# A two-branch attention block on one core: the instruction order planned with another model of the shared port, and another last norm

## The chip, the cores and the metric

The program runs on one core of a Trainium2 chip, alone. The metric is the device time of one execution in microseconds. The kernel before was timed three times: 430.37, 432.68 and 432.4 us, median 432.4 us. The engines are TensorE (PE, with its weight loads PEld), VectorE (DVE), ScalarE (ACT), GpSimd (POOL) and SyncE (SP, which only issues DMAs).

## What is computed

One residual layer on 512 tokens of width 1024, in float32, cut to what matters here:

```python
h = rmsnorm(x, norm_g)
q_lat, c_kv, k_rope, z_a, q_b, k_b, v_b, z_b, q_idx, k_idx, w_idx, gate_a, gate_b = split(h @ w_in)
# branch A: 8 heads, low-rank latents, dense chunk-causal softmax
q = rmsnorm(q_lat, g_q_lat) @ w_uq;  kv = rmsnorm(c_kv, g_kv_lat) @ w_ukv
y_a = mla_attention(q, kv, rope(k_rope)) * silu(z_a)
# branch B: an indexer scores the keys, each query keeps its best 128, 8 heads with a bias by distance
score = sum_h relu(q_idx[h] @ k_idx.T / sqrt(32)) * w_idx[h] / sqrt(8)
y_b = dsa_attention(q_b, k_b, v_b, top_k(score, 128), rel_bias) * silu(z_b)
merged = sigmoid(gate_a) * (y_a @ w_o_a) + sigmoid(gate_b) * (y_b @ w_o_b)
out = rmsnorm(x + merged @ w_out, final_g)
```

## The kernel before

Every float32 operand of a large product is split into a rounded high part and the rest, and a product is three matmuls (high by high, high by low, low by high; `mm3`). The split is two instructions: ACT rounds (a CAST, written `act`), and DVE or GpSimd subtracts (`lo_part`, a TENSOR_TENSOR). Work is tiled in 128 rows by up to 512 columns; `s0` to `s72` are SBUF slots of 128x512 that all stages share, `raw` four larger buffers for weights that arrive, `ps` the eight PSUM banks. In the names of the trace and of the order, what stands behind an underscore (`s_w`, `s_latraw`) is what the slot holds.

The stages in time: the input, its latents (`latent`: the q latent 384 wide and the kv latent 256 wide, scaled per token and turned by TensorE transposes) and the indexer's q and k; then gates and projections of the normed input, which serve as filling work, beside branch A's heads, the scores of the indexer (`scores`, L841 in the trace) and the choice of the best keys (`topk`, MAX8 and MATCH_REPLACE on DVE); then branch B's heads; then the products with `w_o` and, by a seven-product scheme, with `w_out`; then the last norm (`finish`, `square`, `scale_out`), token tile by token tile, tile 1 last.

Nothing of the order is left to a scheduler at run time. The program is written as some sixty generators, each yielding steps, and a planner (`Flow`) runs them against a model of the chip: a step has a list of engines that could do it with a duration each, the model knows when an engine, a buffer and the shared port are free (`start`, `run`), and the step with the smallest key is emitted next. So the order on each engine is a result of the model's numbers. Each engine then executes its own list strictly in order and waits on semaphores; a wrong guess of the model becomes a wait that holds everything behind it on that engine.

Three parts of the model bear on the change. DVE steps with `pair` (two SBUF inputs, or a fast scaling) and POOL's computing steps share one port: `port` is the time at which the last of them ends, and another may start only then. A choice between engines is biased by `PEARLY`, `pbias` and, after the last top-k, by `LATE`. A thread has a priority, weighted by `BIAS` and for POOL by `YIELD`.

GpSimd also issues some DMAs itself (`pool_dma`, L466: tables, and with `QPOOL = 1` the first of three copies that build each of the indexer's eight q tiles `s_qs`; the other two go through SP, L462). `small_pow` (L402, L410) makes 1/sqrt of a mean for four token tiles: on GpSimd one multiply-add and one power.

In the last norm each half row (tile `t`, half 0 or 1) is read out of PSUM by DVE into `s_xr` (L371), squared and summed by ACT (for the last piece by DVE, L1807), and multiplied by `final_g` (`s_fg`). For half 1, and for tile 1, DVE first makes `s_rg` = row by gain by sqrt(1024), and the scale by 1/norm follows; for half 0 of tiles 0, 2 and 3 DVE does both at once, after the norm is known, and stores `s_xr`.

Of the kernel before, what the change touches and what calls it, by code (L numbers as in the profile page):

```python
# [150 lines left out]
class Flow:  # L151
# [126 lines left out]
def tile_block(ctx: ExitStack, tc: tile.TileContext, a: dict, out: bass.AP, bias_dram: bass.AP):  # L278
# [121 lines left out]
    def small_pow(dst, src, mul):  # L400

        yield Step([("POOL", 0.17, lambda: nc.gpsimd.tensor_scalar(dst.ap, src.ap, mul, EPS, ALU.mult, ALU.add))],  # L402
# [83 lines left out]
    def pool_dma_out(dst, src):  # L486
        step = Step([("POOL", 1.03, lambda: nc.gpsimd.dma_start(dst, src.ap))], [], bufs(src))
# [385 lines left out]
    def bias_table():  # L873
        yield is_done("loads")
# [922 lines left out]
    def finish(t, half, c0, c1, ps, nth, last, keep=False):  # L1797

        r = xr[t, half].all.f[:, c0:c1]
# [4 lines left out]
        if last:  # L1804
# [7 lines left out]
            done.add(("sum", t))
        else:
            spawn(square(t, r, nth), 0)
# [298 lines left out]
```

## Time and profile before

| | |
|---|---|
| runs | 430.37, 432.68, 432.4 us; median 432.4 us |
| the profiled execution | 432.45 us, of which the span of the profile is 430.7 us |
| granted TensorE clock, mean | 0.995 |
| PE busy | 418.3 us, 97% of the span |
| DVE, ACT, POOL busy | 380.3, 258.9, 96.0 us |
| HBM read, written | 50.49 MB, 4.21 MB |

The profile is one execution. Times in its rows are microseconds from the span's start. A timeline row gives the start, the time from the first start to the last end of equal neighbours, the engine and line, the operation, what is written and read, the shape and the count; in brackets the idle time before and what ended it. SPq, POOLq and ACTq are the issuing sequencers; DMA_DIRECT2D is the issue of a DMA. Matmuls are pipelined and their ends are modelled, so that idle time of PE in the rows is less than what a wait costs; the distance from start to start is the better measure.

### The profile page before, as it was taken

The page shows a single profiled execution, that of the slowest core. Times are in us where ns is not written, and L with a number is a line of the kernel's source. Part 1 is how long each engine was busy: PE and PEld are TensorE (multiplying, and loading weights), DVE is VectorE, ACT ScalarE, POOL GpSimd, SP SyncE. Part 2 cuts the span into 40 slices and gives each one's busy share as a digit, 9 for nine tenths or more (in the row PEclk, how much of TensorE's full clock was granted, in tenths as well). Part 3 has the DMA queues.
Part 4 walks back from the last instruction along what each step waited for, and adds up shares of the span by engine and source line. Part 5 has one row for each costly group of instructions (what it writes and reads, how often), then busy time and mean ns, then how long its engine had stood idle before and what let it go on. Part 6 is the DMA issues. An engine that isn't in the chain of part 4 may idle for free.

```text
span 430.7 us, 7067 instructions
## 1 busy us (share of the span) xinstructions
PE 418.3 (97%) x2305; PEld 363.5 (84%) x2305; DVE 380.3 (88%) x818; ACT 258.9 (60%) x585; POOL 96.0 (22%) x118
## 2 busy tenths in 40 slices
PE   9999989999999999999999999999999999999993
PEld 6999768789887888888899987998988888888883
DVE  5778699999999999899677899998899858999996
ACT  5786766658492857658363665674489524346623
POOL 2043746434444444300003001000020000000312
PEclk9999999999999999999999999999999999999997
DMA  8973334634425563372443435255333786548305
GB/s 266 395 262 107 101 102 130 176 118 116 149 67 144 160 154 98 85 217 73 129 135 118 148 119 132 75 153 145 87 98 123 263 325 223 187 158 278 107 2 195
DMA packets 30277, 65.89 MB, mean 153 GB/s; under 512 B 4648, under 2 KB 5688, under 8 KB 30240
## 3 DMA queue, kind: packets, MB, share of 16 engines
q1 hardware_dynamic: 29120, 63.82, 47.7%
q0 software_dynamic: 832, 1.22, 1.1%
q8 instruction: 18, 0.29, 0.3%
q10 hardware_dynamic: 288, 0.39, 0.2%
q14 instruction: 19, 0.16, 0.1%
HBM read 50.49 MB, written 4.21 MB: 127 GB/s over the span
## 4 chain that ended last, share of the span: by engine, by line
PE 51%; DVE 25%; ACT 7%; issue 7%; DMA 5%; POOL 2%; SPq 1%; POOLq 0%; DVEq 0%; ACTq 0%
PE ps L435 45%; PE ps L452 3%; ACT s_p L338 2%; DVE sm L863 2%; DVE mask L864 2%; DMA s_op<-s_op 2%; DVE mask L371 2%; DMA s_raw<-onehot 1%; DVE s_wo L360 1%; DVE s_mg L360 1%; DVE s_pair L360 1%; DVE sm L1513 1%; DVE s_w L360 1%; SPq L462 1%; DVE s_ph L360 1%
## 5 line engine op out<-in xcount | busy, mean ns | idle before, releaser
L435 PE MATMUL ps<-s_h,s_w 128*128 128x512 f32 (+1 forms) x732 | 171.5, 379 | 0.0
L435 PEld LDWEIGHTS ps<-s_h,s_w 128*128 128x128 f32 x732 | 127.8, 189 | 21.6 <-issue 0.2
L329 ACT CAST s_w<-raw 128x512 fp32r<-128x512 f32 (+3 forms) x124 | 71.7, 593 | 28.0 <-DVE raw L360 14.0
L362 POOL TENSOR_TENSOR s_w<-raw,s_w 128x512 fp32r<-128x512 f32 (+2 forms) x34 | 41.5, 1227 | 154.9 <-ACT s_w L329 100.8
L360 DVE TENSOR_TENSOR s_w<-raw,s_w 128x512 fp32r<-128x512 f32 (+2 forms) x90 | 58.1, 661 | 7.7 <-ACT s_w L329 7.4
L435 PE MATMUL ps<-s_ys,s_w 128*128 128x512 f32 x192 | 43.7, 389 | 0.0
L435 PEld LDWEIGHTS ps<-s_ys,s_w 128*128 128x128 f32 x192 | 36.0, 188 | 7.5
L435 PE MATMUL ps<-s_w,s_xg 128*128 128x328 f32 (+1 forms) x192 | 32.9, 324 | 0.2 <-ACT s_rbc L329 0.2
L435 PE MATMUL ps<-s_wo,s_mg 128*128 128x512 f32 (+1 forms) x156 | 33.0, 373 | 0.0
L435 PEld LDWEIGHTS ps<-s_wo,s_mg 128*128 128x128 f32 x156 | 27.6, 188 | 5.2
L435 PEld LDWEIGHTS ps<-s_w,s_xg 128*128 128x128 f32 x192 | 31.4, 188 | 0.6 <-ACT s_rbc L329 0.5
L338 ACT ACTIVATE s_p<-s_p,sm 128x256 f32<-128x256 f32 (+3 forms) x50 | 27.2, 560 | 7.8 <-DVE sm L1610 7.8
L338 ACT ACTIVATE s_p<-ps,sm 128x128 f32<-128x128 f32 (+3 forms) x32 | 16.7, 525 | 15.7 <-DVE sm L1513 15.5
L864 DVE MATCH_REPLACE8 mask<-sm,mask 128x256 f32<-128x256 f32 (+2 forms) x48 | 25.8, 540 | 0.0
L863 DVE MAX8 sm<-mask 128x8 f32<-128x256 f32 (+2 forms) x48 | 25.1, 547 | 0.1
L452 PE MATMUL ps<-ident,s_p 128*128 128x128 f32 x160 | 22.8, 273 | 0.0
L329 ACT COPY s_tmp<-ps 64x512 f32<-64x512 f32 (+1 forms) x18 | 10.1, 562 | 18.9 <-PE ps L435 18.8
L435 PE MATMUL ps<-s_lat,s_w 128*128 128x512 f32 x78 | 21.0, 397 | 0.0
L452 PEld LDWEIGHTS ps<-ident,s_p 128*128 128x128 f32 x160 | 18.6, 140 | 2.5
L435 PE MATMUL ps<-s_hs,s_w 128*128 128x256 f32 x144 | 20.0, 285 | 0.0
L360 DVE TENSOR_TENSOR s_ph<-ps,s_ph 128x512 fp32r<-128x512 f32 (+1 forms) x32 | 18.5, 611 | 0.6 <-ACT s_ph L329 0.6
L435 PEld LDWEIGHTS ps<-s_hs,s_w 128*128 128x128 f32 x144 | 18.4, 191 | 0.2
(198 smaller groups left out, 759.1 us busy)
## 6 DMA issues: line engine op xcount, KB each, us to landing
raw<-w_out SPq DMA_DIRECT2D x18, 512.0 KB, 4.2
s_op<-s_op SPq DMA_DIRECT2D x36, 128.0 KB, 2.4
raw<-w_ga SPq DMA_DIRECT2D x8, 512.0 KB, 4.6
raw<-w_gb SPq DMA_DIRECT2D x8, 512.0 KB, 3.8
raw<-w_o SPq DMA_DIRECT2D x16, 256.0 KB, 5.4
s_x<-xT SPq DMA_DIRECT2D x8, 256.0 KB, 4.9
s_xn<-x SPq DMA_DIRECT2D x8, 256.0 KB, 5.6
bias_scratch<-s_sig SPq DMA_DIRECT2D x8, 256.0 KB, 3.7
```

Of the source, the lines that this page charges most:

```text
L329: nc.scalar.copy(dst.ap, src.ap)
L338: nc.scalar.activation(dst.ap, src.ap, func, **kw)
L360: opts.append(("DVE", 0.07 + 0.00104 * x.n, lambda: nc.vector.tensor_tensor(dst.ap, x.ap, y.ap, op=op)))
L362: opts.append(("POOL", 0.15 + 0.0021 * x.n, lambda: nc.gpsimd.tensor_tensor(dst.ap, x.ap, y.ap, op=op)))
L371: lambda: nc.vector.scalar_tensor_tensor(dst.ap, x.ap, sc(s), y.ap, op0=op0, op1=op1))],
L435: nc.tensor.matmul(ps.ap, l.ap, r.ap, start=start and i == 0, stop=stop and i == len(pairs) - 1, skip_group_check=more)
L452: nc.tensor.transpose(d.ap, s.ap, ident.tile)
L462: return Step([("SP", n / 360000.0, lambda: nc.sync.dma_start(d, s))], bufs(dst), bufs(src))
L863: yield Step([("DVE", t, lambda: nc.vector.max(m8.tile, work.tile))], [m8], [work])
L864: yield Step([("DVE", t + 0.068, lambda: nc.vector.match_replace(work.tile, m8.tile, work.tile, MARK))], [work], [m8])
L1513: yield Step([("DVE", 0.07 + 0.00104 * n, lambda: nc.vector.tensor_reduce(mx.tile[:, 1:2], ps.tile[:, :n], op=ALU.max, axis=AX.X, negate=T ...
```

## The change

Five things change. The first is the model of the port: a step that would take the port from the other engine while it is still held, or is free for less than 0.01, is marked down by `SWITCH`, so that the holder's next step goes first; `BIAS` is halved.

```diff
-        self.port = 0.0
+        self.port, self.holder = 0.0, None
...
+                        change = SWITCH * (self.shares(t.req, eng) and eng != self.holder and s < self.port + 0.01)
+                        key = (max(s, self.due) + change + BIAS * t.prio + t.off + YIELD * self.shares(t.req, eng) * (eng == "POOL"), t.prio)
...
-                    self.port = end
+                    self.port, self.holder = end, eng
...
-BIAS = 0.004
+BIAS = 0.002
...
+SWITCH = 0.1
```

The second is GpSimd's DMAs: an issue costs the model 0.53 in place of 1.03, and a load from DRAM lands 2.5 later; no copy of the q tiles goes through GpSimd (`QPOOL = 0`), and the bias table begins when the rope keys are done (`BIAS_AT`) in place of when the loads are issued. Other numbers of the planner change with them.

```diff
-        step = Step([("POOL", 1.03, lambda: nc.gpsimd.dma_start(dst.ap, s))], bufs(dst), bufs(src))
+        step = Step([("POOL", 0.53, lambda: nc.gpsimd.dma_start(dst.ap, s))], bufs(dst), bufs(src))
+        step.late = 0.0 if isinstance(src, View) else 2.5
...
-        yield is_done("loads")
+        yield is_done("loads", BIAS_AT)
...
-QPOOL = 1
+QPOOL = 0
...
-PTOPK = 18.0
+PTOPK = 12.0
...
-LATE = 1.5
-PSUMS = 4.0
+LATE = 0.75
+PSUMS = 10.0
...
+BIAS_AT = 'kpe'
```

The third is the norm: the multiply-add of `small_pow` may be done by ACT or DVE, no longer by GpSimd.

```diff
-        yield Step([("POOL", 0.17, lambda: nc.gpsimd.tensor_scalar(dst.ap, src.ap, mul, EPS, ALU.mult, ALU.add))],
+        yield Step([("ACT", 0.1, lambda: nc.scalar.activation(dst.ap, src.ap, AF.Copy, scale=mul, bias=EPS)),
+                    ("DVE", 0.1, lambda: nc.vector.tensor_scalar(dst.ap, src.ap, mul, EPS, ALU.mult, ALU.add))],
                    bufs(dst), bufs(src))
         yield power(dst)
```

Both the second and the third show in GpSimd's list. Here is what stands there before, from the norm of the kv latents (`sm_78`) to that of the q latents (`sm_80`) and the first subtractions of weights:

```order
L402 TENSOR_SCALAR sm_78<-sm_77 128x4
L410 TENSOR_TENSOR sm_78<-sm_78,neghalf 128x4
L466 DMA s_qs_700<-s_th_510 32x384
L393 TENSOR_SCALAR s_latraw_519<-s_latraw_519,sm_78 128x256
L393 TENSOR_SCALAR s_latraw_530<-s_latraw_530,sm_78 128x256
L402 TENSOR_SCALAR sm_80<-sm_79 128x4
L410 TENSOR_TENSOR sm_80<-sm_80,neghalf 128x4
L362 TENSOR_TENSOR s_th_751<-s_tmp_748,s_th_750 128x384
L466 DMA s_qs_774<-s_th_750 32x384
L362 TENSOR_TENSOR s_w_757<-raw_67,s_w_756 128x384
L362 TENSOR_TENSOR s_w_799<-raw_67,s_w_798 128x384
```

And the same place after (lines have moved by two or three: 413 is the power, 469 the DMA, 395 the scaling, 364 the subtraction):

```order
L413 TENSOR_TENSOR sm_78<-sm_78,neghalf 128x4
L469 DMA s_raw_497<-chunk 4x512
L469 DMA qhi_72<-s_oh_498 4x512
L469 DMA qhi_73<-s_oh_498 4x512
L469 DMA qhi_74<-s_oh_498 4x512
L469 DMA qhi_75<-s_oh_498 4x512
L413 TENSOR_TENSOR sm_80<-sm_80,neghalf 128x4
L395 TENSOR_SCALAR s_latraw_716<-s_latraw_716,sm_80 128x384
L395 TENSOR_SCALAR s_latraw_734<-s_latraw_734,sm_80 128x384
L395 TENSOR_SCALAR s_latraw_751<-s_latraw_751,sm_80 128x384
L364 TENSOR_TENSOR s_w_769<-raw_67,s_w_768 128x384
L364 TENSOR_TENSOR s_w_803<-raw_67,s_w_802 128x384
```

The two multiply-adds and the copies to `s_qs` have left GpSimd; three of the four scalings of the q latents came to it (before, DVE did three and ACT one), ahead of the subtractions of weights; the kv latents are scaled by ACT.

SP's list has the eight copies more. Where branch B's first head is made ready (`s_op` are its operands, built of copies of the rope keys `kpeh`, `kpel` and of rotated values), it reads before:

```order
L462 DMA s_op_1640<-s_op_1623 64x512
L462 DMA raw_66<-w_kb 128x1024
L462 DMA s_op_1642<-s_op_1625 64x512
L462 DMA s_op_1572<-s_qpe_994 32x512
L462 DMA qhi_73<-s_qpe_993 32x512
L462 DMA s_op_1604<-s_qpe_994 32x512
L462 DMA s_op_1623<-kpeh 36x512
L462 DMA s_op_1625<-kpel 32x512
```

And after:

```order
L465 DMA s_op_1625<-s_op_1571 64x512
L465 DMA s_op_1532<-kpeh 36x512
L465 DMA bias_scratch<-s_sig_1675 128x512
L465 DMA s_op_1571<-kpel 32x512
L465 DMA s_op_1596<-kpeh 36x512
L465 DMA s_op_1625<-kpel 32x512
L465 DMA raw_66<-w_kb 128x1024
```

The load of `w_kb`, which stood among the copies, stands behind them; the store of a bias tile, `s_sig`, stands among them.

TensorE's list is rearranged between the latents and the end of branch A. One place, the scores of the indexer late in it, among the matmuls of a projection (`s_h`), before:

```order
L841 MATMUL ps_96<-s_qs_715,s_qs_880 128x384
L841 MATMUL ps_95<-s_qs_715,s_qs_774 128x512
L435 MATMUL ps_94<-s_h_543,s_w_950 128x512
L435 MATMUL ps_94<-s_h_544,s_w_950 128x512
L435 MATMUL ps_94<-s_h_543,s_w_952 128x512
L841 MATMUL ps_93<-s_qs_715,s_qs_919 128x384
```

After, the last score 384 wide (L845 now) stands earlier, among the values of branch A (`s_w` by `s_lat`, 256 columns):

```order
L438 MATMUL ps_96<-s_w_919,s_lat_724 128x256
L438 MATMUL ps_96<-s_w_921,s_lat_724 128x256
L438 MATMUL ps_96<-s_w_919,s_lat_725 128x256
L845 MATMUL ps_94<-s_qs_732,s_qs_626 128x384
L438 MATMUL ps_96<-s_w_919,s_lat_724 128x256
```

No score stands among the projections that follow it and come before the first logits; the three that are left (512 wide) come some 250 instructions later.

The fourth is the last norm. `final_g` is scaled by sqrt(1024) once, on ACT; every half row gets an `s_rg` = row by gain, as a TENSOR_TENSOR; all scalings by 1/norm come after that, half 0 on ACT or DVE; the last row's two column parts count as buffers of their own, and the last sum of squares writes its products into `s_rg` in place of a scratch buffer.

```diff
+            yield act(f.all.f, f.all.f, AF.Copy, scale=D ** 0.5)
...
-        if half == 0 and t != 1:
-            return
-        if (t, half) not in rg:
-            rg[t, half] = yield slot("rg")
-        yield stt(rg[t, half].all.f[:, c0:c1], r, D ** 0.5, fg[half].all.f[:, c0:c1], ALU.mult, ALU.mult)
+        yield soon(tt(y, r, fg[half].all.f[:, c0:c1], ALU.mult, ("DVE",) if last or t == 1 and half else BOTH))
...
-        if t != 1:
-            x = xr[t, 0].all.f
-            yield ts(rs[:, 2:3], rs[:, 0:1], D ** 0.5, None, ALU.mult)
-            yield stt(x, x, rs[:, 2:3], fg[0].all.f, ALU.mult, ALU.mult)
-            yield dma(out[TOK[t], 0:512], x)
-        yield Until(lambda: all(("g", t, i) in done for i in range(int(t != 1), count)))
-        for half, engs in ((0, ("DVE",)), (1, ("ACT",))):
+        yield Until(lambda: all(("g", t, i) in done for i in range(count)))
+        for half, engs in ((0, ("DVE",) if t == 1 else ("ACT",) if t == 0 else ("ACT", "DVE")), (1, ("ACT",))):
```

The fifth is priorities at that end: tile 1's `finish`, `square` and `scale_out` go ahead of the others' (-5 against 0, 5 and -1). DVE's list at its end, before (`ps_99` and `ps_95` hold the last two column parts of tile 1, `s_xr_4424` is tile 0):

```order
L371 SCALAR_TENSOR_TENSOR s_xr_4436<-ps_99,s_xr_4436 128x256
L371 SCALAR_TENSOR_TENSOR s_rg_4767<-s_xr_4436,s_fg_4501 128x256
L379 TENSOR_SCALAR sm_89<-sm_89 128x1
L371 SCALAR_TENSOR_TENSOR s_xr_4436<-ps_95,s_xr_4436 128x256
L371 SCALAR_TENSOR_TENSOR s_xr_4424<-s_xr_4424,sm_89,s_fg_4497 128x512
L379 TENSOR_SCALAR sm_78<-ssf_121 128x1
L1807 ISA junk,sm_78<-s_xr_4436,sm_78 128x256
L1807 ISA sm_78 128x1
L371 SCALAR_TENSOR_TENSOR s_rg_4767<-s_xr_4436,s_fg_4501 128x256
L390 TENSOR_SCALAR s_rg_4583<-s_rg_4583,sm_78 128x512
```

And after:

```order
L373 SCALAR_TENSOR_TENSOR s_xr_4436<-ps_97,s_xr_4436 128x256
L381 TENSOR_SCALAR sm_91<-ssf_120 128x1
L362 TENSOR_TENSOR s_rg_4759<-s_xr_4436,s_fg_4547 128x256
L373 SCALAR_TENSOR_TENSOR s_xr_4436<-ps_98,s_xr_4436 128x256
L381 TENSOR_SCALAR sm_83<-ssf_121 128x1
L1821 ISA s_rg_4759,sm_83<-s_xr_4436,sm_83 128x256
L1821 ISA sm_83 128x1
L362 TENSOR_TENSOR s_rg_4759<-s_xr_4436,s_fg_4547 128x256
L392 TENSOR_SCALAR s_rg_4582<-s_rg_4582,sm_83 128x512
```

The multiplication of tile 0 by its norm and gain, which stood between the last reading of PSUM and the last sum of squares, is gone from DVE; ACT has two scalings more ahead of its last one. The count of matmuls is the same on both sides.

More of the change, by code (lines that the diff above doesn't have):

```diff
@@ L249, in run @@
                 if self.shares(step, eng):
-                    self.port = end
+                    self.port, self.holder = end, eng
                 if step.moves:
                     self.dma = max(self.dma, end + (1.0 if eng == "POOL" else 0.8)) + step.moves
-                    end = self.dma + (1.25 if s < 3.0 else 1.0)
+                    end = self.dma + (1.25 if s < 3.0 else 1.0) + step.late
             for b in step.ins:
@@ L486, in pool_dma_out @@
     def pool_dma_out(dst, src):
-        step = Step([("POOL", 1.03, lambda: nc.gpsimd.dma_start(dst, src.ap))], [], bufs(src))
+        step = Step([("POOL", 0.53, lambda: nc.gpsimd.dma_start(dst, src.ap))], [], bufs(src))
         step.moves = 4.0 * src.n * src.ap.shape[0] / 360000
@@ L1797, in finish @@
     def finish(t, half, c0, c1, ps, nth, last, keep=False):
-        r = xr[t, half].all.f[:, c0:c1]
+        pieces = t == 1 and half == 1
+        if pieces and not isinstance(xr[t, half], Split):
+            xr[t, half] = Split(xr[t, half], 256)
+        r = xr[t, half][:, c0:c1].f
+        if (t, half) not in rg:
+            rg[t, half] = None
+            y = yield slot("rg")
+            rg[t, half] = Split(y, 256) if pieces else y
+        yield Until(lambda: rg[t, half] is not None)
+        y = rg[t, half][:, c0:c1].f
         yield stt(r, ps[:, c0:c1], 0.5, r, ALU.mult, ALU.add)
@@ L1807, in finish @@
             step = Step([("DVE", 0.16 + 0.00104 * r.n, lambda: nc.vector.tensor_tensor_reduce(
-                junk.tile[:, : r.n], r.ap, r.ap, op0=ALU.mult, op1=ALU.add, scale=1.0, scalar=rs.tile[:, 1:2],
-                accum_out=rs.tile[:, 0:1]))], [junk, rs], bufs(r) + [rs])
+                y.ap, r.ap, r.ap, op0=ALU.mult, op1=ALU.add, scale=1.0, scalar=rs.tile[:, 1:2],
+                accum_out=rs.tile[:, 0:1]))], bufs(y) + [rs], bufs(r) + [rs])
             step.count = 2
+            step.pair = True
             yield step
@@ L1813, in finish @@
         else:
[L1814 to L1819 removed]
+            spawn(square(t, r, nth), -5 if t == 1 else -1)
+        yield soon(tt(y, r, fg[half].all.f[:, c0:c1], ALU.mult, ("DVE",) if last or t == 1 and half else BOTH))
         done.add(("g", t, nth))
@@ L1840, in scale_out @@
         yield power(rs[:, 0:1])
-        if t != 1:
-            x = xr[t, 0].all.f
-            yield ts(rs[:, 2:3], rs[:, 0:1], D ** 0.5, None, ALU.mult)
-            yield stt(x, x, rs[:, 2:3], fg[0].all.f, ALU.mult, ALU.mult)
-            yield dma(out[TOK[t], 0:512], x)
-        yield Until(lambda: all(("g", t, i) in done for i in range(int(t != 1), count)))
-        for half, engs in ((0, ("DVE",)), (1, ("ACT",))):
-            if half == 0 and t != 1:
-                continue
-            x = rg[t, half].all.f
+        yield Until(lambda: all(("g", t, i) in done for i in range(count)))
+        for half, engs in ((0, ("DVE",) if t == 1 else ("ACT",) if t == 0 else ("ACT", "DVE")), (1, ("ACT",))):
+            x = getattr(rg[t, half], "whole", rg[t, half]).all.f
             yield scale_by(x, x, rs[:, 0:1], engs)
@@ L1943, in output @@
                     yield mm3(ps[:, c0:c1], tuple(v[:, i * P : i * P + P] for v in left4[k]), cut(right[3, k], slice(c0, c1)), False, k == 3, True)
-                spawn(finish(i, 1, c0, c1, ps, 1 + (c0 > 0), c0 > 0), 0)
-            spawn(scale_out(i, 2 + i), 0)
+                spawn(finish(i, 1, c0, c1, ps, 1 + (c0 > 0), c0 > 0), -5 if i else 0)
+            spawn(scale_out(i, 2 + i), -5 if i else 5)
     outs = [(p, c) for p, n in ((1, 2), (7, 4), (2, 2), (6, 2), (5, 4), (4, 2), (3, 2)) for c in range(n)]
```

3 lines of the change are left out of this document (1 added, 2 removed).

## The prediction

> **What bounds the kernel now.** I read the page first, then the busy time of each engine in stretches of 10 us, then what PE waits for, then the timeline around each of its waits.
>
> ```profile
> span 430.7 us, 7067 instructions
> PE 418.3 (97%) x2305; PEld 363.5 (84%) x2305; DVE 380.3 (88%) x818; ACT 258.9 (60%) x585; POOL 96.0 (22%) x118
> ```
>
> PE is busy for 97% of the span. The number of matmuls does not change, so the change can give only what PE now loses in waits and what lies behind its last matmul. How fast a matmul of 512 columns goes when nothing is waited for is read from a long run of them:
>
> ```profile
> 327.97 13.85 PE L435 MATMUL ps<-s_h,s_w 128*128 128x512 f32 x60
> ...
> 341.65 3.56 PE L435 MATMUL ps<-s_ys,s_w 128*128 128x512 f32 x15
> ```
>
> Sixty starts take 341.65 - 327.97 = 13.68 us, 0.228 us each. Where a group takes longer from start to start, PE was held up. The view of waits, for PE, names these holds besides one at the start of the program:
>
> ```profile
> PE ps L452 <- DVE s_latraw L390: 1.3, 1, 1.3
> ...
> PE ps L841 <- DVE s_qs L360: 0.9, 1, 0.9
> PE ps L841 <- DVE s_op L371: 0.8, 1, 0.8
> PE ps L435 <- DVE s_ph L360: 0.5, 1, 0.5
> PE ps L1528 <- DMA s_op<-kpeh: 0.3, 1, 0.3
> ```
>
> The releasing engine is DVE in four of the five. Three stretches (the columns are PE, PEld, DVE, ACT and POOL busy with their counts, the granted clock, the share of the DMA engines, GB/s):
>
> ```profile
> 50.00:60.00 10.00, 7.80 (x38) 5.38 (x37) 8.26 (x13) 7.87 (x17) 6.52 (x9) 1.00 0.45 158
> ...
> 70.00:80.00 10.00, 9.21 (x54) 7.87 (x53) 10.00 (x15) 8.01 (x17) 6.29 (x5) 1.00 0.50 143
> ...
> 150.00:160.00 10.00, 10.00 (x56) 8.60 (x55) 9.79 (x21) 6.62 (x13) 4.32 (x5) 1.00 0.59 147
> ```
>
> PE misses 2.2 us at 50 to 60 and 0.8 at 70 to 80, and nothing at 150 to 160, where DVE nevertheless has work for 9.8 of 10 us. So the middle of the program has two engines near their limit: PE leads, and DVE has hardly any slack to give.
>
> **The change part by part.** The latents come first, where two of the holds are.
>
> ```profile
> 46.30 0.35 DVE L390 TENSOR_SCALAR s_latraw<-s_latraw,sm 128x256 f32<-128x256 f32 x1 [1.21 <-POOL sm L410]
> ...
> 46.88 0.94 POOL L393 TENSOR_SCALAR s_latraw<-s_latraw,sm 128x256 f32<-128x256 f32 x2
> ...
> 48.40 0.60 PE L452 MATMUL ps<-ident,s_latraw 128*128 128x128 f32 x4
> ...
> 50.58 1.64 PE L435 MATMUL ps<-s_h,s_w 128*128 128x512 f32 x6
> 50.67 0.19 POOL L402 TENSOR_SCALAR sm<-sm 128x4 f32<-128x4 f32 x1 [2.85 <-ACT junk L338]
> ...
> 50.95 1.04 POOL L410 TENSOR_TENSOR sm<-sm,neghalf 128x4 f32<-128x4 f32 x1
> ...
> 52.39 0.68 DVE L360 TENSOR_TENSOR s_qs<-ps,s_qs 32x512 fp32r<-32x512 f32 x1
> ...
> 53.10 3.29 DVE L390 TENSOR_SCALAR s_latraw<-s_latraw,sm 128x384 f32<-128x384 f32 x3
> ...
> 53.13 0.56 PE L841 MATMUL ps<-s_qs,s_qs 96*128 96x256 f32 x2 [0.91 <-DVE s_qs L360]
> ...
> 53.53 1.97 POOL L362 TENSOR_TENSOR s_w<-raw,s_w 128x384 fp32r<-128x384 f32 x2
> ...
> 54.23 0.27 PE L452 MATMUL ps<-ident,s_latraw 128*128 128x128 f32 x1
> ...
> 55.78 0.99 PE L452 MATMUL ps<-ident,s_latraw 128*128 128x128 f32 x3 [1.28 <-DVE s_latraw L390]
> ...
> 56.53 0.95 PE L435 MATMUL ps<-s_h,s_w 128*128 128x512 f32 x3
> ```
>
> Place 1, the first scores. Six matmuls from 50.58 at 0.228 would end at 51.95; the scores start at 53.13, when DVE has subtracted the low part of the key `s_qs` (52.39 and 0.68). Lost: 1.18. After the change the scores stand later in PE's list, behind more projection work, and the key's subtraction is not later on DVE. I take -1.0, bounds -1.18 and 0.
>
> Place 2, the q latents. Four transposes and what lies between them take 56.53 - 54.23 = 2.30; four that wait for nothing take at most the 0.60 of the row at 48.40. Lost: 1.70. The cause is the row at 53.10: three scalings take 3.29 on DVE, 1.10 each, where one of two thirds of that size took 0.35 at 46.30; beside them GpSimd runs its two subtractions of weights, 1.97. After the change GpSimd does the three scalings, ahead of its subtractions. Its own two at 46.88 took 0.47 each, so three half as wide again take at most 3 x 0.71 = 2.1. The power ends at 51.99, so they are done by about 54.1, and the transposes follow them with no more than a few tenths of waiting. I take -1.6, bounds -1.7 and +1.5. The upper end has a reason of its own: in GpSimd's list five DMA issues now stand ahead of this power, and the last of them carry what ACT casts from a load that GpSimd itself issues.
>
> ```profile
> s_raw<-chunk POOLq DMA_DIRECT2D x2, 8.0 KB, 7.1
> ```
>
> That load takes 7.1 us to land. The cast of it on ACT stands ahead of the squares of the q latents; if the load is issued under 7 us ahead of the cast, ACT waits with the squares, the power and the scalings queued behind it. What hides it is that the norm of the kv latents, which it follows, can run early (its scalings stand ahead of eight casts of the input on ACT now), and the 2.85 that GpSimd sat idle ahead of 50.67. The multiply-add that leaves GpSimd saves 50.95 - 50.67 = 0.28 on this path twice and costs ACT or DVE about as much as the 0.19 of its row: nothing.
>
> The model of the port is made for the following rows, further ahead.
>
> ```profile
> 41.40 1.89 DVE L360 TENSOR_TENSOR s_h<-s_x,s_h 128x512 fp32r<-128x512 f32 x3
> ...
> 42.85 2.29 POOL L402 TENSOR_SCALAR sm<-sm 128x4 f32<-128x4 f32 x1
> ```
>
> The multiply-add of four numbers a partition takes 0.19 at 50.67 and 2.29 at 42.85, beside a row of subtractions on DVE that went on through it at 1.89 / 3 = 0.63 each. So GpSimd waited through several DVE instructions, not one: the holder goes on, which is what `SWITCH` assumes. In a sentence by itself: the Trainium skill, page "SBUF — State Buffer", section "Who interferes with whom", says that whoever issues first has the shared pair for the whole instruction and the other fully blocks; the full block agrees with these rows, but a lock of one instruction would let GpSimd in after one.
>
> Place 3, scores among the projections.
>
> ```profile
> 76.75 2.38 DVE L371 SCALAR_TENSOR_TENSOR s_qpe<-s_tmp,s_qpe 128x512 fp32r<-128x512 f32 x2
> 76.92 1.66 POOL L362 TENSOR_TENSOR s_w<-raw,s_w 128x512 fp32r<-128x512 f32 x1 [2.29 <-ACT s_w L329]
> ...
> 78.12 0.87 PE L435 MATMUL ps<-s_h,s_w 128*128 128x512 f32 x3
> ...
> 79.78 0.45 PE L841 MATMUL ps<-s_qs,s_qs 96*128 96x384 f32 x1 [0.79 <-DVE s_op L371]
> ```
>
> Three matmuls from 78.12 end at 78.80; the score starts at 79.78, as its bank is read by DVE late, behind the two instructions that shared the port with GpSimd. Lost: 0.98. After, no score stands there; the last come among the heads. I take -0.9, bounds -0.98 and 0.
>
> Place 4, operand copies of branch B's first head.
>
> ```profile
> 130.28 7.72 PE L435 MATMUL ps<-s_h,s_w 128*128 128x512 f32 x33
> ...
> 138.27 0.33 PE L1528 MATMUL ps<-s_op,qhi 100*128 100x128 f32 x1 [0.27 <-DMA s_op<-kpeh]
> ```
>
> Thirty-three matmuls from 130.28 end at 137.80, and PE starts at 138.27: 0.47 lost to a copy that SP issues. In SP's list the load of `w_kb` no longer stands among these copies, but a store does, and a store waits for what it stores, with the copies queued behind it. I take -0.2, bounds -0.5 and +0.5.
>
> Place 5, meetings at the port in the late heads.
>
> ```profile
> 259.61 2.31 DVE L390 TENSOR_SCALAR s_p<-s_p,sm 128x128 f32<-128x128 f32 x4
> 259.95 1.36 POOL L362 TENSOR_TENSOR s_w<-raw,s_w 128x512 fp32r<-128x512 f32 x1 [29.77 <-ACT s_w L329]
> ```
>
> Four small scalings take 2.31 on DVE across a subtraction of 1.36 on GpSimd. At the 0.35 or less of such a scaling alone they would take at most 1.4, so such a meeting costs DVE about 0.9 to 1.1. GpSimd's subtraction stands at the same place after the change. I take 0; if it went, at most the 0.5 that PE waits for `s_ph`, and what DVE carries on from here, together -1.3; if it gets worse, one meeting more, +1.0.
>
> Place 6, the end.
>
> ```profile
> 424.25 0.74 DVE L371 SCALAR_TENSOR_TENSOR s_xr<-s_xr,sm,s_fg 128x512 f32<-128x512 f32 x1
> ...
> 425.72 0.67 POOL L410 TENSOR_TENSOR sm<-sm,neghalf 128x1 f32<-128x1 f32 x1 [1.95 <-DVE sm L1807]
> ...
> 426.42 0.72 ACT L338 ACTIVATE s_rg<-s_rg,sm 128x512 f32<-128x512 f32 x1 [1.73 <-POOL sm L410]
> ```
>
> The 0.74 of tile 0 stands on the chain from the last reading of PSUM to the last sum of squares, the power and the last scaling. It is gone from DVE; ACT has two more scalings of 0.72 ahead of its last, and it was idle for 1.73, which hides both in the main. I take -0.5, bounds -0.8 and +0.2.
>
> GpSimd's eight copies of the q tiles go to SP.
>
> ```profile
> 32.34 2.52 SPq L462 DMA_DIRECT2D s_qs<-s_th  x4
> ```
>
> At 2.52 / 4 = 0.63 each, eight more are 5 us of issuing; loads of weights and the bias store are queued behind them. SP only issues, and at 50 to 60 the DMA engines are busy for 0.45 of the time, so I cost this at nothing; without that cover the next weights come late, and the price is some of place 2's bound. The two scalings of `final_g` on ACT, 0.72 each at most, lie far ahead of their use: nothing.
>
> One term is left: rearranged lists make new meetings. DVE has none to spare at 70 to 80 and hardly any at 150 to 160, so a meeting there can reach PE at up to 1.1. I take +0.8, less than one; bounds 0 and 5.5 (five).
>
> The sum: -1.0 - 1.6 - 0.9 - 0.2 + 0 - 0.5 + 0.8 = -3.4. Against this execution, 432.45 (span 430.7 and 1.75 around it, within 0.1 of the median of the runs), that is 429.0.
>
> **The rivals.** First, DVE bounds the middle: what PE gains at places 1 to 3 it waits for in the heads, because DVE's work up to 180 is as long as before. For it speaks 9.8 of 10 at 150 to 160; against it, that DVE itself gets back what it lost to GpSimd at 53.10, some 1.7 (3.29 against three times one and a half times 0.35). What stays is the end: 432.45 - 0.5 = 431.9.
>
> Second, the holder does not go on and the port is a lock per instruction. Then the model's marks reorder without removing a meeting, each one costs at most one instruction of the other (1.36 at 259.95), the holds move and stay, and again only the end is gained: 431.9. In a sentence by itself: this is what the rule of the Trainium skill's page "SBUF — State Buffer" would make of it. The row of 2.29 speaks against; the rows at 259.61 and 259.95 would allow it.
>
> Third, more goes than I count: the meeting at 259.61 goes with the rest, place 5's -1.3, no new ones come, -0.8, and the other places reach their lower bounds (0.18 + 0.10 + 0.08 + 0.3 + 0.3, together -1.0): 429.0 - 3.1 = 425.9. Against it: GpSimd's subtraction stands where it stood.
>
> Fourth, slower: fewer issues of DMAs leave GpSimd free, and the planner gives it scalings and subtractions in the heads, where DVE is full. Each meeting delays DVE by 1.1, and PE behind it. The gain of 4.2 without that term is eaten by four; six give 432.45 - 4.2 + 6.6 = 434.8. For it: GpSimd has a few instructions more after; against: the new mark puts the holder's steps together, and GpSimd was 22% busy.
>
> **How the numbers follow.** Forecast 429.0, chance 0.46 (its own range 427.2 to 430.2); first rival 0.24; second 0.06; third 0.12; fourth 0.12. The range leaves out half of the third and half of the fourth: 425.9 to 433.4. About half a per cent, 2.2 us, is what a measurement of this kernel can tell from no change. Faster by more than that means under 430.2: the forecast, the third, nothing else of weight: 0.57. Same: the first two, with a part of the fourth's smaller cases, 0.31. Slower, over 434.6: 0.12, from the fourth and place 2's upper end.
>
> **What would show it.** PE's row of waits for `s_latraw` is gone, and the transposes of the q latents follow within 1 us in all; the three scalings stand on GpSimd with 0.5 to 0.7 each; from 50 to 60 PE is busy for over 9.3. At 78 no score waits. In DVE's list no 0.74 stands between the last PSUM reading and the last sum of squares, and the last scaling on ACT waits for GpSimd's power still. DVE's scalings of over 0.5 at 128 columns would show new meetings. It is wrong if a hold for ACT's cast of the small load shows ahead of the q latents, if PE is busy for less than 9.9 at 150 to 160, where it was full, or if its waits for DVE move there with the same sum.

## The result, and the profile after

The changed kernel takes 426.52 us (median of 4 runs, 425.98 to 427.43), the kernel before 432.37 (4 runs beside it, 430.37 to 432.68). The ratio is 0.9877, interval 0.9842 to 0.9911: faster by 1.2%. Forecast were 429.0 (0.8%), so the sign was right and the gain in the runs was 5.9 in place of 3.4. The time lies inside the whole range, 425.9 to 433.4, but below the forecast's own 427.2 to 430.2, between it and the third rival. The profiled execution of after is the slowest of its four, 427.43, with a span of 425.7. In later comparisons the kernel before had medians of 431.4 to 431.7 over 48 runs, so that the execution whose profile was read for the prediction, 432.45, was a rather slow one; against those medians the gain would be about 5. That matters below.

The head of the page of after:

```profile
span 425.7 us, 7077 instructions
PE 416.6 (98%) x2305; PEld 362.8 (85%) x2305; DVE 375.4 (88%) x809; ACT 266.2 (63%) x597; POOL 94.1 (22%) x109
```

Because the matmuls are the same in number and end with the same group of 36, the start of that group tells everything that TensorE lost before it. From the timeline of before, then of after:

```profile
418.01 5.75 PE L435 MATMUL ps<-s_wo,qhi 128*128 128x512 f32 x36
```
```profile
413.07 5.75 PE L438 MATMUL ps<-s_wo,qhi 128*128 128x512 f32 x36
```

It starts 4.94 earlier, and the spans differ by 5.0: in these two profiles all of the gain is waiting that TensorE no longer does, and nothing comes from the end. Here is what is left of PE's waits for other engines (besides 1.0 at the start and 0.2 for `s_rbc` at 29.5, which stand in both profiles), and four stretches of after (columns as in the prediction):

```profile
PE ps L1532 <- DMA s_op<-kpel: 0.3, 1, 0.3
PE ps L438 <- DVE s_ph L362: 0.2, 1, 0.2
PE ps L438 <- DVE s_last L362: 0.2, 1, 0.2
```
```profile
50.00:60.00 10.00, 10.00 (x54) 8.44 (x53) 9.66 (x17) 8.63 (x20) 6.11 (x8) 1.00 0.39 132
...
70.00:80.00 10.00, 10.00 (x55) 8.06 (x54) 10.00 (x19) 6.62 (x15) 6.70 (x8) 1.00 0.67 159
80.00:90.00 10.00, 9.71 (x47) 7.84 (x45) 10.00 (x35) 3.65 (x10) 3.56 (x4) 1.00 0.59 191
...
150.00:160.00 10.00, 10.00 (x55) 8.62 (x54) 9.73 (x23) 4.89 (x14) 3.83 (x3) 1.00 0.54 163
```

The two large holds at the latents and the one at the scores are gone, PE is full from 50 to 80, and 150 to 160 is as full as it was. The latents in the timeline of after:

```profile
33.76 1.57 POOL L413 TENSOR_TENSOR sm<-sm,neghalf 128x4 f32<-128x4 f32 x1 [1.44 <-DVE sm L405]
...
44.62 2.01 POOL L469 DMA_DIRECT2D qhi<-s_oh  x4 [8.73 <-ACT s_oh L331]
...
48.79 1.03 POOL L413 TENSOR_TENSOR sm<-sm,neghalf 128x4 f32<-128x4 f32 x1 [2.16 <-DVE sm L405]
49.07 3.00 PE L438 MATMUL ps<-s_h,s_w 128*128 128x512 f32 x12
...
49.92 1.72 POOL L395 TENSOR_SCALAR s_latraw<-s_latraw,sm 128x384 f32<-128x384 f32 x3
51.91 0.46 PE L845 MATMUL ps<-s_qs,s_qs 96*128 96x256 f32 x2
52.90 0.60 PE L455 MATMUL ps<-ident,s_latraw 128*128 128x128 f32 x4
53.26 0.47 PE L845 MATMUL ps<-s_qs,s_qs 96*128 96x512 f32 x1
```

The power of the q latents ends at 49.82, where it ended at 51.99, the three scalings take 1.72 on GpSimd and are done before the first transpose, and the four transposes wait for nothing. The power of the kv latents ends at 35.3. In the timeline of before it ended at 46.27, for reasons that the prediction did not follow up:

```profile
38.45 0.46 ACT L329 CAST s_oh<-s_raw 64x320 fp32r<-64x320 f32 x1 [1.51 <-DMA s_raw<-onehot]
...
40.24 2.02 POOL L466 DMA_DIRECT2D qhi<-s_oh  x4 [6.61 <-ACT s_oh L329]
...
46.30 0.51 ACT L338 ACTIVATE s_latraw<-s_latraw,sm 128x256 f32<-128x256 f32 x1 [2.45 <-POOL sm L410]
```

ACT waited 1.51 for a load of the one-hot table (it belongs to the bias table); GpSimd, with its DMA issues at the head of its list, 6.61 for a cast that stands behind that one on ACT; then ACT 2.45 for the power that stood behind those issues on GpSimd. The squares of the q latents come behind that on ACT.

### The profile page after: what moved, and what is told of

Read it like the earlier page. It is cut to its first block, busy times and chain, and to the rows that moved or that the text cites. A ratio compares the mean times of both kernels' runs of the same rounds, so it can differ in the third digit from the quotient of the medians.

```text
span 425.7 us, 7077 instructions
## 1 busy us (share of the span) xinstructions
PE 416.6 (98%) x2305; PEld 362.8 (85%) x2305; DVE 375.4 (88%) x809; ACT 266.2 (63%) x597; POOL 94.1 (22%) x109
## 4 chain that ended last, share of the span: by engine, by line
PE 70%; DVE 17%; ACT 4%; issue 3%; DMA 3%; SPq 1%; POOL 0%; POOLq 0%; DVEq 0%; ACTq 0%
PE ps L438 62%; PE ps L455 4%; ACT s_p L340 2%; DVE s_mg L362 1%; DVE s_wo L362 1%; PE ps L1533 1%; PE ps L1534 1%; DVE s_pair L362 1%; PE ps L1532 1%; DVE s_w L362 1%; SPq L465 1%; DVE s_xr L373 1%; DMA s_er<-w_kvl 1%; DVE s_wsum L362 1%; DVE s_pair L373 1%
## 5 line engine op out<-in xcount | busy, mean ns | idle before, releaser
L364 POOL TENSOR_TENSOR s_w<-raw,s_w 128x512 fp32r<-128x512 f32 (+2 forms) x39 | 47.9, 1236 | 143.5 <-ACT s_w L331 129.0
L362 DVE TENSOR_TENSOR s_w<-raw,s_w 128x512 fp32r<-128x512 f32 (+2 forms) x85 | 54.7, 659 | 5.7 <-ACT s_w L331 4.9
L340 ACT ACTIVATE s_p<-s_p,sm 128x512 f32<-128x512 f32 (+3 forms) x56 | 31.1, 574 | 3.7 <-DVE sm L1614 3.3
L331 ACT CAST s_ph<-ps 128x512 fp32r<-128x512 f32 (+1 forms) x32 | 15.8, 537 | 4.5 <-PE ps L455 4.4
```

The source lines that it names most:

```text
L331: nc.scalar.copy(dst.ap, src.ap)
L340: nc.scalar.activation(dst.ap, src.ap, func, **kw)
L362: opts.append(("DVE", 0.07 + 0.00104 * x.n, lambda: nc.vector.tensor_tensor(dst.ap, x.ap, y.ap, op=op)))
L364: opts.append(("POOL", 0.15 + 0.0021 * x.n, lambda: nc.gpsimd.tensor_tensor(dst.ap, x.ap, y.ap, op=op)))
```

## The experiments

In the experiments on before and after, the planner's steps are left as they are and one is emitted on another engine, or emission is kept back until the planner's step of a later number (`HOLD = {step: until}`), so that nothing else moves; three kernels change a number of the planner and one undoes part of the program, and these get another order. The diffs are shortened to the option that changes. The letters A to F stand for the theories that the expectations name; C, for one, is that DVE bounds the middle. In the table: median, ratio to the runs of before beside it with its interval, PE's busy time from 50 to 60 in the profile, and the start of the last 36 matmuls.

| kernel | us | ratio | 50 to 60 | last group |
|---|---|---|---|---|
| before | 432.37 | | 7.80 | 418.01 |
| after | 426.52 | 0.9877 (0.9842 to 0.9911) | 10.00 | 413.07 |
| b_pool3 | 429.65 | 0.9962 (0.9947 to 0.9977) | 9.56 | 414.26 |
| b_mad | 432.02 | 1.0019 (0.9995 to 1.0043) | 9.22 | 415.92 |
| b_order | 429.70 | 0.9956 (0.9934 to 0.9978) | 9.22 | 415.65 |
| b_late | 431.32 | 1.0006 (0.9978 to 1.0034) | 8.85 | 416.23 |
| b_oh | 430.78 | 0.9975 (0.9957 to 0.9993) | 9.71 | 414.47 |
| b_all | 428.41 | 0.9920 (0.9890 to 0.9951) | 10.00 | 414.06 |
| a_dve3 | 428.36 | 0.9922 (0.9894 to 0.9951) | 9.04 | 413.48 |
| a_oldend | 427.26 | 0.9895 (0.9865 to 0.9926) | 10.00 | 412.81 |
| a_switch0 | 426.80 | 0.9889 (0.9862 to 0.9917) | 10.00 | 413.39 |
| a_qpool | 428.20 | 0.9920 (0.9889 to 0.9951) | 10.00 | 413.78 |
| a_bias | 430.79 | 0.9982 (0.9962 to 1.0002) | 8.92 | 416.18 |

The profile is one execution, and the last two columns carry its luck; the median decides where they differ.

**b_pool3**: before, with the q latents' scalings that DVE did on GpSimd.

```diff
-   ("DVE", t, lambda: nc.vector.tensor_scalar(...))     # latent, width 384
+   ("DVE", t, lambda: nc.gpsimd.tensor_scalar(...))
```

> The kernel before with one edit: the three scalings of the q latents that DVE did are done by GpSimd, at the place where they were emitted (behind one subtraction and one DMA issue, ahead of the two subtractions of weights); every other list is unchanged. Theory A, GpSimd's queue: the q latents are late because their norm is late, and GpSimd starts the scalings only at about 53.5, so they end at about 55.2 in place of 56.4; PE gets back 0.9 to 1.2 of what it loses between 50 and 60. Theory B, the port at the scalings, as predicted: place 2 loses 0.3 or less in place of 1.70, PE gets back 1.4 to 1.7. Theory C, DVE bounds the middle: whatever is got back is lost again by 180, and the time is that of the kernel before within 0.3.

```profile
52.23 1.70 POOL L775 TENSOR_SCALAR s_latraw<-s_latraw,sm 128x384 f32<-128x384 f32 x3
...
52.85 0.38 PE L452 MATMUL ps<-ident,s_latraw 128*128 128x128 f32 x2
...
54.08 0.94 PE L435 MATMUL ps<-s_h,s_w 128*128 128x512 f32 x3
```

The three take 1.70 in place of 3.29, and the time falls by 1.6 (0.38%; the interval is 1.0 to 2.3, so it holds B's 1.4 to 1.7 and A's 0.9 to 1.2). The trace speaks for A's size: the transposes take 54.08 - 52.85 = 1.23 in place of 2.30, 1.1 less, and two of them still wait 0.2 each. Another 0.4 stands at 78, where the score waits 0.4 in place of 0.8. So the meeting of the scalings with the subtractions has its price, but place 2 is not cleared by moving the scalings alone. The gain reaches the end: against C.

**b_mad**: before, with the multiply-add of the kv latents' norm on DVE.

```diff
-   ("POOL", 0.17, lambda: nc.gpsimd.tensor_scalar(dst, src, 1/256, EPS, mult, add))
+   ("POOL", 0.17, lambda: nc.vector.tensor_scalar(dst, src, 1/256, EPS, mult, add))
```

> The kernel before with one edit: the multiply-add of the kv latents' norm (2.29 us on GpSimd at 42.85) is done by DVE; all else is as before. Theory A: the power ends about 2 us earlier, ACT's wait of 2.45 ahead of its kv scaling shrinks to about 0.4, the squares, the power and the scalings of the q latents follow about 2 us earlier, and PE gets back 1.5 to 2.2 between 50 and 60. Theory B: the three scalings still meet the two subtractions, so PE gets back 0.3 or less. Theory C: got back and lost again, the time as before.

```profile
42.35 0.16 DVE L770 TENSOR_SCALAR sm<-sm 128x4 f32<-128x4 f32 x1
...
42.59 2.01 POOL L410 TENSOR_TENSOR sm<-sm,neghalf 128x4 f32<-128x4 f32 x1 [1.55 <-DVE sm L770]
44.64 0.51 ACT L338 ACTIVATE s_latraw<-s_latraw,sm 128x256 f32<-128x256 f32 x1 [2.35 <-POOL sm L410]
```

Nothing is gained (1.0019). The multiply-add fell from 2.29 to 0.16, but it stands behind a subtraction on DVE, and the power behind it takes 2.01 in place of 1.04, beside the same row of subtractions; ACT waits 2.35, about as before. The 2.29 was thus not a price of that instruction but of the time at which GpSimd asked for the port. A's expectation failed here, and this part of the change by itself is worth nothing.

**b_order**: before, with the norm of the kv latents ahead of five DMA issues in GpSimd's list.

```diff
+HOLD = {247: 279, 255: 279, 261: 279, 266: 279, 269: 279}
```

> The kernel before with one edit: in GpSimd's list the norm of the kv latents (multiply-add and power) stands ahead of the five DMA issues that wait for ACT's cast of a small load, in place of behind them; all else is as before. Theory A: the power ends at about 38 to 39 in place of 46.3, ACT no longer waits 2.45 for it, the q latents' squares come 2 to 2.5 earlier, and PE gets back 1.8 to 2.6 of the 2.9 that it loses at places 1 and 2. Theory B: 0.3 or less. Theory C: got back and lost again, the time as before.

```profile
51.06 3.31 DVE L403 TENSOR_SCALAR s_latraw<-s_latraw,sm 128x384 f32<-128x384 f32 x3
```

The time falls by 1.9 (0.44%), as A has it and against B, though the one-hot load was as late in its profile as in that of before (ACT waits 1.60 for it), and the three scalings still take 3.31. So two causes are shown, by an edit each: the port at the scalings, and the place of the norm in GpSimd's queue.

**b_late**: before, with a score six matmuls later and the load of `w_kb` behind the copies.

```diff
+HOLD = {519: 528, 522: 528, 829: 863}
```

> The kernel before with two edits, far apart: the last score that is 384 wide stands six matmuls later in TensorE's list (place 3), and the load of w_kb stands behind the copies of the rope keys in SyncE's list (place 4); all else is as before. If the holds are local and PE is the bound: the 0.98 at 78 and 0.5 to 0.8 of the 0.80 at 137 to 139 go, and the last matmul ends 1.4 to 1.8 earlier. Theory C, DVE bounds the middle: the same holds vanish, but PE waits for DVE elsewhere between 80 and 180, and the last matmul ends 0 to 0.5 earlier.

```profile
36.98 0.46 ACT L342 CAST s_oh<-s_raw 64x320 fp32r<-64x320 f32 x1
...
78.38 0.44 PE L854 MATMUL ps<-s_qs,s_qs 96*128 96x384 f32 x1 [0.81 <-DVE s_op L384]
```

It misses: the score that was moved is the next one, and the one that waits still waits 0.81. PE is busy all of 130 to 140 here, but also in b_pool3, b_mad, b_order and b_oh, where the load of `w_kb` was not moved; so place 4's loss belonged to the first execution, and the edit says nothing on it. The row at 36.98 shows something else: the table's load has landed in time, without an edit. Place 1's wait is then absent, too, and the busy time from 50 to 60 is 8.85 against 7.80. So place 1's loss, like place 4's, was in part one of the first execution.

**b_oh**: before, with the cast of the table's second half later on ACT. In the trace it stands behind four more casts, not two.

```diff
+HOLD = {238: 254}
```

> The kernel before with one edit: ACT's cast of the second half of the one-hot table stands two casts later in ACT's list; all else is as before (two names of slots apart). Theory D, the late load: the table's load is issued by GpSimd at 32.06 and lands between 36.7 and 38.4 in the runs seen so far; where it is late ACT waits up to 1.6 us for it, everything of the latents is late by as much, and PE loses it at places 1 and 2. Then no wait of ACT for that load is left, PE loses 2.1 to 2.4 between 50 and 60 in every run (3.43 in the first profile), the slowest runs go, and the median falls by 0.3 to 1.0. If that load is not the cause: 3.4 between 50 and 60, median and spread as before.

```profile
38.73 0.62 ACT L342 CAST kpeh<-s_raw 4x512 fp32r<-4x512 f32 x1 [1.01 <-DMA s_raw<-chunk]
...
40.62 0.19 POOL L415 TENSOR_SCALAR sm<-sm 128x4 f32<-128x4 f32 x1
```

The time falls by 1.1 (0.25%, interval 0.3 to 1.9), where D has 0.3 to 1.0. The slowest run is 431.9, where before had 433.4, so the slow end is gone, as D has it; nine of the ten lie within 1.4, and one is faster, 428.95. But ACT now waits 1.01 for the next load from GpSimd's queue. The profile is of that fastest run. There the multiply-add comes before DVE's row and takes 0.19 in place of 2.29; in b_late, where it comes at 41.39, it takes 2.33. A shift of under a microsecond decides the meeting.

**b_all**: before, with all of these moves at once except b_mad's, and with the score that waits moved in place of the next one. The three scalings are on GpSimd, as in b_pool3.

```diff
+HOLD = {247: 279, 255: 279, 261: 279, 266: 279, 269: 279, 509: 514, 512: 514, 829: 863, 238: 254}
```

> The kernel before with all the small moves at once: norm of the kv latents ahead of the DMA issues on GpSimd, the q latents' three scalings on GpSimd, the one-hot cast two casts later, the score that waits at 78 six matmuls later, the load of w_kb behind the copies. If the sum of the holds is the whole change: PE loses under 0.5 between 50 and 60 and under 0.5 at 70 to 80, nothing new comes, and the time is within 1 us of the changed kernel's (426.5), 0.9 to 1.2% under before. Theory C, DVE bounds the middle: PE gets back the 3 to 4 us by 80 and loses half or more of it in waits for DVE between 80 and 180: 429.5 or more. If the planner's new order does something that single moves do not: 428 to 429.

```profile
PE ps L1545 <- DMA s_op<-kpel: 0.4, 1, 0.4
PE ps L465 <- POOL s_p L406: 0.3, 1, 0.3
```

Faster by 0.80%, 3.3 to 3.5 of the 5 to 6. The holds at the latents and at 78 are gone, and two small ones have come, 0.4 for a copy at 83.4 and 0.3 for a scaling of GpSimd at 92.7, in the heads. A few moves in the lists are thus worth about two thirds of the change. Some of what PE gets back is lost again, but 428.41 is clear of C's 429.5. By the third expectation the remaining third is the planner's other order as a whole; no run shows which part of it.

**a_dve3**: after, with the three scalings back on DVE.

```diff
-   ("POOL", t, lambda: nc.gpsimd.tensor_scalar(...))    # latent, width 384
+   ("POOL", t, lambda: nc.vector.tensor_scalar(...))
```

> The changed kernel with one edit: the three scalings of the q latents go back to DVE, at the place where they were emitted; all else is as after. Theory B, the port at the scalings, as predicted: they meet GpSimd's subtractions again, and PE loses 1.3 to 1.7 at the transposes. Theory A, the norm comes early enough: the power ends at 49.8 and GpSimd's subtractions start only at 51.6, so DVE does the scalings at about 0.5 each with its other work between; PE loses 0 to 0.5, and the time is within 0.5 us of the changed kernel's.

```profile
53.16 0.99 POOL L364 TENSOR_TENSOR s_w<-raw,s_w 128x384 fp32r<-128x384 f32 x1 [0.94 <-ACT s_w L331]
53.25 1.11 DVE L779 TENSOR_SCALAR s_latraw<-s_latraw,sm 128x384 f32<-128x384 f32 x1
...
54.42 0.33 PE L455 MATMUL ps<-ident,s_latraw 128*128 128x128 f32 x1 [0.96 <-DVE s_latraw L779]
```

Slower than after by 1.8 in the medians, which is B's size. The trace lies between the theories: the first two scalings take 0.41 and 0.58, as A has it; the third stands behind DVE's shuffle, meets a subtraction, takes 1.11, and PE waits 0.96 for it. From the first transpose to the next group it is 54.50 - 52.97 = 1.53, where after has 0.36, so PE loses 1.2, a little under B's 1.3. The meeting at the port is there again, with one scaling in place of three.

**a_oldend**: after, with the last norm of before (the fourth and fifth part of the diff undone).

> The changed kernel with the last norm of before (parts four and five of the change undone: gain within the scaling, tile 0 done by one DVE instruction, old priorities). As predicted: the chain from the last matmul to the end is 0.5 longer, 7.4 in place of 6.9. From the two traces: it is 6.9 in both, since after the change the chain goes through ACT's square, which stands behind two scalings; then the time is that of the changed kernel within 0.3.

```profile
419.44 0.75 DVE L373 SCALAR_TENSOR_TENSOR s_xr<-s_xr,sm,s_fg 128x512 f32<-128x512 f32 x1
420.11 0.42 DVE L373 SCALAR_TENSOR_TENSOR s_xr<-ps,s_xr 128x256 f32<-128x256 f32 x1
```

From the start of the last group to the end of the span it is 12.69 in before, 12.63 in after and 426.2 - 412.81 = 13.39 here; the median is 0.7 over after's, with intervals that overlap. The second expectation fails, and the first has the direction but not the reason: under the new numbers the planner puts the 0.75 of tile 0 ahead of the last reading of PSUM, which starts 1.55 after the last matmul. Before, it stood behind it. So the new end avoids a loss of about 0.7 that the new numbers would have brought, and is worth next to nothing against before.

**a_switch0**: after, with the preference for the port's holder off.

```diff
-SWITCH = 0.1
+SWITCH = 0.0
```

> The changed kernel planned with SWITCH at 0, so that the holder of the port is no longer preferred; GpSimd's list up to its 35th row stays as after, later lists differ. Theory E, the port's model carries little: the latents stay as after (PE loses under 0.5 between 50 and 60), and the time is within 1.0 us of the changed kernel's (426.5), above or below by what new meetings cost. Theory F, the holder's preference is what pays: 429 or more, with DVE or GpSimd instructions stretched beside each other ahead of PE's waits.

426.80 against 426.52: the intervals of the ratios overlap almost wholly, and PE is full from 50 to 60. Theory E stands: the mark for the port's holder, after which the change is named, cannot be measured in its time. (The halved `BIAS` stayed as after.)

**a_qpool**: after, with the first copy of each q tile through GpSimd.

```diff
-QPOOL = 0
+QPOOL = 1
```

> The changed kernel planned with QPOOL at 1: the first copy of each q tile goes through GpSimd again, and in the plan five DMA issues that wait for ACT's cast stand ahead of the power of the kv latents' norm, as before the change. Theory A, GpSimd's queue: ACT waits for that power, the latents are late again, PE loses 1 to 2.5 between 50 and 60, and the time is 428 to 429.5. If the queue does not matter and the rest of the plan pays: within 0.7 of 426.5.

428.20 has the time that A gave, and not its reason: PE is busy all of 50 to 60 (10.00), although the five issues stand ahead of the power again. Its profile has two waits for the split input `s_xg` at 4 to 7 us, 0.35 and 0.62, that the profile of after lacks. But such waits come and go between executions (none in before, 0.8 in b_mad, whose order is the same there), so where the 1.7 goes is not settled.

**a_bias**: after, with the bias table begun with the loads, as before.

```diff
-BIAS_AT = 'kpe'
+BIAS_AT = 'loads'
```

> The changed kernel planned with the bias table begun when the loads are issued, as before: the one-hot loads stand early in GpSimd's list, and ACT casts them among the latents. Theory D, the late load: ACT waits up to 1.5 us for them in some runs, the spread of the runs grows beyond 1.5 us, and the median is 0.5 to 1.5 over 426.5. If their place does not matter: within 0.5 of 426.5, spread as in the changed kernel.

```profile
PE ps L1532 <- DMA s_op<-kpel: 1.9, 1, 1.9
PE ps L845 <- DVE s_qs L362: 0.6, 1, 0.6
PE ps L845 <- DVE s_lat L373: 0.5, 1, 0.5
```

430.79: 4.3 over after, beyond what any theory gave, and not clear of before. Scores wait 0.6 and 0.5 from 50 to 60, and the first logits 1.9 for a copy that SP issues about 2.8 later than in after. The runs spread from 429.7 to 432.1 (2.4; after 1.5). ACT does not wait for the table here, so D's mechanism is not what shows; the plan around it is another one from the input on, and how much is the table's and how much that order's is not told apart.

**port**: none of the layer's work; DVE and GpSimd meet on purpose (the code is shortened).

```python
for i in range(1, n + 1):
    nc.vector.tensor_tensor(o[i], x, y, op=ALU.subtract)   # or tensor_scalar, or x in PSUM
nc.gpsimd.tensor_scalar(small, o[1][:, :4], 2.0, 1.0, ALU.mult, ALU.add)
```

> None of the reference's work is done: DVE and GpSimd meet on purpose, on 128x512 tiles, once with two SBUF inputs on DVE (n = 1, 2, 4, 8 in a row), with the fast scaling (4, 8), with one input in PSUM (4, 8), and a multiply-add of four numbers on GpSimd becomes ready behind the first of the row; then GpSimd runs 1, 2, 3 subtractions in a row and DVE has one of 128 columns ready behind the first. If the holder goes on, as the new model has it: the multiply-add lasts until the row ends, about 0.2, 0.8, 2.1, 4.6 for n = 1, 2, 4, 8, growing by 0.63 for each instruction; with PSUM inputs 0.2; DVE's instruction lasts until GpSimd's row ends. If the port is let go after each instruction: 0.2 to 0.9 whatever n, and DVE waits at most one subtraction.

The timeline: DVE's rows of 4 and 8 subtractions with GpSimd's multiply-add under each, that beside 8 fast scalings, that beside 8 with PSUM, and GpSimd's row of 3 with DVE's instruction:

```profile
6.66 2.49 DVE L298 TENSOR_TENSOR o<-xin,yin 128x512 f32<-128x512 f32 x4
7.43 0.57 POOL L312 TENSOR_SCALAR tt<-o 128x4 f32<-128x4 f32 x1 [0.88 <-DVE o L298]
...
9.14 4.90 DVE L298 TENSOR_TENSOR o<-xin,yin 128x512 f32<-128x512 f32 x8
9.90 4.18 POOL L312 TENSOR_SCALAR tt<-o 128x4 f32<-128x4 f32 x1 [1.91 <-DVE o L298]
...
16.11 0.30 POOL L312 TENSOR_SCALAR fast<-o 128x4 f32<-128x4 f32 x1 [1.11 <-DVE o L301]
...
21.59 0.19 POOL L312 TENSOR_SCALAR bank<-o 128x4 f32<-128x4 f32 x1 [2.27 <-DVE o L304]
...
30.10 3.75 POOL L319 TENSOR_TENSOR big<-xin,yin 128x512 f32<-128x512 f32 x3
31.40 1.33 DVE L321 TENSOR_TENSOR pool<-big,yin 128x128 f32<-128x128 f32 x1 [2.09 <-POOL big L319]
```

Neither theory is right throughout, and each row is one meeting in one execution. Beside eight subtractions GpSimd waits out the row, 4.18 until 14.08; beside four it is let in when the instruction that runs ends, 0.57, and beside two as well; fast scalings let it in, 0.30; with an input in PSUM there is no wait, 0.19. DVE beside GpSimd's row of three waits 1.33, one instruction and not the row. The Trainium skill, page "SBUF — State Buffer", section "Who interferes with whom", has the first comer hold the shared pair for the whole instruction (it says so of DVE's two-port modes) and says nothing of rows. One instruction is what GpSimd as holder shows, and the row of eight goes beyond it. Why four let go and eight do not stays open.

## Why the prediction was right or wrong, point by point

- **The bound**: right. In the two profiles all of the gain is PE's waits, 4.94, and it is kept: PE is full at 150 to 160, and the first rival, DVE as the bound of the middle, falls with b_pool3, b_order and b_all.
- **Places 1 and 2**, forecast -2.6: the scores start within 0.1 of twelve free matmuls (49.07 + 12 x 0.228 = 51.81, and 51.91) and the transposes take 0.36 where they took 2.30, together -3.0. The price of 1.70 had left the four transposes the 0.60 of their row; from start to start they need 0.36. The port at the scalings is shown from both sides (b_pool3 -1.6, a_dve3 +1.8 in the medians; 1.1 and 1.2 at the transposes). What failed is the step that put place 1 down to DVE's subtraction of the key: the key was late because ACT was, behind the one-hot load and the power in GpSimd's queue. With either of these gone (b_late, b_order) the score does not wait, so that its 1.0 was partly luck: the profile read was one of an execution with a late load. "Nothing" was right for the multiply-add (b_mad), but the norm's earlier place in GpSimd's queue (b_order, -1.9) and the later bias table had no price at all; the idle times of ACT and GpSimd ahead of those rows would have shown them. The wait that was feared, for the small load ahead of the q latents, did not come: GpSimd's issues stand there after a wait of 8.73, done by 46.6, 2.2 ahead of the power.
- **Place 3**, forecast -0.9: PE's idle time falls by 0.79 at 70 to 80 (from 9.21 busy) and rises by 0.14 at 80 to 90, where PE waits 0.3 for a copy.
- **Place 4**, forecast -0.2: the first profile lost 0.4 at 130 to 140, but four kernels with the same order there lost nothing. It was a term read from one execution.
- **Place 5**, forecast 0: right. The meeting stands in after as it stood:

```profile
254.89 2.31 DVE L392 TENSOR_SCALAR s_p<-s_p,sm 128x128 f32<-128x128 f32 x4
255.24 1.35 POOL L364 TENSOR_TENSOR s_w<-raw,s_w 128x512 fp32r<-128x512 f32 x1 [29.77 <-ACT s_w L331]
```

  The wait for `s_ph`, 0.2 in place of 0.5, is another place, at 320.85 before and 316.25 after. There, too, DVE's scalings meet a subtraction of GpSimd in both profiles (2.30 and 2.12 for the row). The new model of the port has not removed either meeting.
- **Place 6**, forecast -0.5: 0.06 at the end of the span. The instruction is gone, and another wait has taken its place:

```profile
419.04 0.42 DVE L373 SCALAR_TENSOR_TENSOR s_xr<-ps,s_xr 128x256 f32<-128x256 f32 x1
419.16 0.40 ACT L340 ACTIVATE junk<-s_xr 128x256 f32<-128x256 f32 x1
...
419.69 0.21 DVE L381 TENSOR_SCALAR sm<-ssf 128x1 f32<-128x1 f32 x1 [0.23 <-ACT junk L340]
```

  ACT's square of the last piece but one stands behind two of the added scalings, and DVE waits for it ahead of the last sum. The step "it was idle for 1.73, which hides both" looked at ACT's idle time ahead of the last scaling, not ahead of the square.
- **New meetings**, forecast +0.8: none that PE feels beyond the 0.3 at 80 to 90. This and the places' sizes, with the 0.2 at `s_ph`, bring -3.4 to about -4.4. Some 0.6 of the profiles' 5.0 is not placed, and the last 0.9 up to the medians' 5.9 shows in no profile, since the execution profiled after the change was its slowest. The number is close to the third rival's 425.9, but its mechanism did not come: the meeting at 259 stayed.
- **The second rival**, a lock per instruction: half right on the port (a row of four lets GpSimd in, a row of eight does not; the 2.29 before stood beside two rows of three, 41.40 to 45.09, of which the prediction shows the first), wrong on the time: the gain is there with the preference for the holder off (a_switch0).

## What to carry to other kernels

Where an engine waits, follow the wait back through the queues: a small power behind DMA issues that wait for a cast that waits for a load cost TensorE about two microseconds, some ten later. When a change bears the name of one idea and moves six numbers, plan it once more with that idea alone switched off, and freeze the order to test a single move. Read a stall of half a microsecond in two profiles of the same order before it becomes a term.

## What the runs showed of the hardware

A load from DRAM that GpSimd issues lands late and unevenly. In the view of DMA issues (KB, then the median us from issue to landing, here of two), before and then after, where some are issued at other times:

```profile
s_raw<-onehot POOLq DMA_DIRECT2D x2, 80.0 KB, 5.3
...
s_raw<-chunk POOLq DMA_DIRECT2D x2, 8.0 KB, 7.1
```
```profile
s_raw<-onehot POOLq DMA_DIRECT2D x2, 80.0 KB, 2.6
s_raw<-chunk POOLq DMA_DIRECT2D x2, 8.0 KB, 4.0
```

The Trainium skill, page "DMA: Bandwidth & Descriptors", section "Anatomy of one DMA — SWDGE (gpsimd) path", gives 2.0 us and bytes over 436 KB per us, an estimate of 2.0 for 8 KB; these rows have 4.0 to 7.1. Between executions with the same order at that place ACT's wait for the one-hot load was none (b_mad, b_late), 0.80 (b_pool3), 1.51 (before) or 1.60 (b_order). The runs of the kernel before spread over 3 us; that no run of b_oh, which moves the cast, is over 431.9 speaks for this load as one reason and does not show it.
